# Key and query products put in runs of one array shape in two attention stages, and two constants stored as full tiles

## The chip, the cores and the metric

The kernel runs on one core of a Trainium2 chip. The metric is the device time of one execution in microseconds, lower is better. The engines are named as in the profile: PE is TensorE's matmul, PEld its weight load (the stationary operand), DVE VectorE, ACT ScalarE, POOL GpSimd, and SP the engine that issues most DMAs. The arrays are float32. Where the code splits a value into a high and a low part of type float32r, it multiplies these parts separately and adds the products.

## The reference

Two transformer layers for 512 tokens of width 1024. The first is a hybrid of a neighbourhood attention (8 heads of 64), a bidirectional gated delta rule (4 heads of 128), an output projection and a mixture of 64 experts. The second joins an mLSTM (4 heads of 256), a short convolution, a stick-breaking attention (16 heads of 64), gates, and an MLP of width 4096. The two parts that the change is about, cut to what matters:

```python
def row_block(args):                       # neighbourhood attention, one row of the grid
    r, q_row = args
    r0 = jnp.clip(r - kh // 2, 0, rows - kh)
    k_win = lax.dynamic_slice_in_dim(kg, r0, kh, axis=0)[:, :, :, col_idx]
    v_win = lax.dynamic_slice_in_dim(vg, r0, kh, axis=0)[:, :, :, col_idx]
    logits = jnp.einsum('bhqd,rbhqcd->bhqrc', q_row, k_win) * scale + bias
    p = jax.nn.softmax(logits.reshape(b_, h_, GRID_W, kh * WIN_W), axis=-1)
    return jnp.einsum('bhqrc,rbhqce->bqhe', p.reshape(b_, h_, GRID_W, kh, WIN_W), v_win)

def block(args):                           # stick-breaking attention, one block of queries
    qblk, start = args
    mask = key_pos[None, :] < q_pos[:, None]
    z = jnp.einsum('bhqd,bshd->bhqs', qblk, kf)
    log_beta = jax.nn.log_sigmoid(z)
    log_1m = jnp.where(mask, log_beta - z, 0.0)
    cum = jnp.cumsum(log_1m, axis=-1)
    a = jnp.where(mask, jnp.exp(log_beta + cum[..., -1:] - cum), 0.0)
    return jnp.einsum('bhqs,bshd->bqhd', a, vf)
```

## The kernel before

The program runs through the layers in order: input projections, the delta rule's preparation, the neighbourhood attention together with the delta rule's scan, the output projection and the routing, the experts, and then the second layer. Most of the work is dense projections, which the text calls jobs: weights come by DMA into a ring of buffers, ACT and DVE split them into a high and a low part (lines 160 and 161), and PE makes 24 matmuls of 128x512 for each block of 128 output columns (`fm_mm`, line 255).

**Who sets the order.** A scheduler orders the instructions on each engine's queue, from the order in the program and its own estimate of when operands are ready. Where the code says `manual_schedule` for PE, PE's queue keeps the program's order. The stick-breaking stage is such a place; the neighbourhood attention is not. In both, a generator of small steps is mixed with another one by hand: `pad` takes a step's figure as the amount of dense work to place behind it. In the stick-breaking stage, dense jobs (line 255) are put between the steps of `sb_group`, six jobs for each group of two pairs, eight for the last. In the neighbourhood attention the steps of `na_attn` are put between those of the scan, `dn_scan` (its matmuls are on lines 1023 to 1125).

**Neighbourhood attention** (`na_attn`, `na_pair`, `na_out`, lines 711 to 797). There are four blocks of 128 queries and eight heads, taken in pairs: 16 calls of `na_pair`, two of them in flight at a time. A block sees two or three blocks of keys (`nb`), so a head's logits have 256 or 384 columns; two of the four blocks have each. The queries and keys of the pair's two heads lie in the partitions 0 to 63 and 64 to 127 of the same tiles. For each head the kernel makes the product of queries and keys (line 743: 64 rows contracted, float32, which PE carries out as two instructions), adds the mask as a product with the identity (line 747: 128 rows, bfloat16), and reads the sum with the bias on DVE (line 750). Then come the exponentials on ACT (759), transposes (767), and the products with the values (775). The logits' accumulators are taken from `pacc`, which has four; the scan takes its own from the same four.

**Stick-breaking** (`sb_stack`, `sb_pair`, lines 1838 to 1927). The 16 heads are taken in eight pairs. For a pair the low and high parts of the queries and keys are stacked: `Q` holds, for each head e, the high part of the queries in its own 64 partitions and the low part in the other 64; `K` the high part of the keys in both; `Kl` the low part of the keys, head 0 in partitions 0 to 63 and head 1 in 64 to 127. So one product of 128 rows (line 1868) gives high times high plus high times low, and one of 64 rows (line 1870) the third term. The logits z of a head are triangular and lie in four regions of 512, 384, 256 and 128 columns, in three accumulators for each head:

```python
for i in range(4):
    b, c, n = self.REG[i]
    for e in range(2):
        o = slice(64 * e, 64 * e + 64)
        ks = slice(i * 128, i * 128 + 128)
        TE.matmul(z[e][b][:, c:c + n], K[:, e, ks], Q[:, e, i * 128:512],
                  start=(i != 3), stop=False, skip_group_check=True)
        TE.matmul(z[e][b][:, c:c + n], Kl[o, ks], Q[o, e, i * 128:512],
                  start=False, stop=False, skip_group_check=True)
```

These 16 matmuls are followed by eight of the causal mask (line 1875, bfloat16, 128 columns each). Then ACT and DVE work out the softplus and split it (lines 1880 to 1893; the low half of `sb_hl` is made on line 1887), with dense jobs on PE meanwhile, and line 1904 (eight matmuls with the triangle `ntri`), 1908 to 1913 (with the constant `none`) and 1923 (with the values) follow for each head.

**Constants** (`b2_consts`). `oner` holds ones and `none` minus ones. Both are one column of 128 partitions, and are read as a stationary operand of 128x128 by a broadcast along the free axis. `none` is used on lines 1908 to 1913 (128 products) and `oner` on line 2065 for the accumulator `ml_pd` (32 products); the same line makes `ml_pn` with a full tile as the stationary operand.

Of the kernel before, what the change touches and what calls it, by code (L numbers as in the profile page):

```python
# [10 lines left out]
F32 = mybir.dt.float32  # L11
F32R = mybir.dt.float32r
# [4 lines left out]
OP = mybir.AluOpType  # L17
# [6 lines left out]
NEG = -1.0e30  # L24
# [57 lines left out]
class Kern:  # L82
# [648 lines left out]
    def na_pair(self, cb, g, block, po, sm):  # L731
        TE, VE, SE, na = self.TE, self.VE, self.SE, self.na
        kb0, nb, (s0, st) = block
        mx = na.tile([128, 2], F32, name="na_mx", tag="na_mx", bufs=2)
        lps, es, pTs = [], [], []
        v = lambda a: a.rearrange("p (r k) -> p r k", r=8)
        for i in range(2):
            h = 2 * g + i
            hp, o = h // 2, 64 * (h % 2)
            lp = na.tile([128, 384], F32, name="na_lp", tag="na_lp", bufs=3)[:, :nb * 128]  # L740
            pl = self.pacc.tile([128, 384], F32, name="na_l", tag=self.atag)[:, :nb * 128]

            TE.matmul(pl, self.qT[o:o + 64, hp, cb, :],
                      self.kT[o:o + 64, hp, kb0 * 128:(kb0 + nb) * 128]
                      .rearrange("p (n r k) -> p r n k", n=nb, r=8), start=True, stop=False)
            mk = self.mk[:, None, s0:s0 + st * (nb - 1) + 1:st, :].to_broadcast([128, 8, nb, 16])
            TE.matmul(pl, self.idb, mk, start=False, stop=True)
            base = self.braw[:, h, 16 * (kb0 - cb + 1):16 * (kb0 - cb + 1) + 1]
            bias = bass.AP(tensor=base.tensor, offset=base.offset, ap=[list(base.ap[0]), [31, 8], [1, 16 * nb]])
            VE.tensor_tensor_reduce(out=v(lp), in0=v(pl), in1=bias, scale=1.0, scalar=NEG,  # L750
                                    op0=OP.add, op1=OP.max, accum_out=mx[:, i:i + 1])
            lps.append(lp)
            if i == 0:
                yield 0.3 * nb
        VE.tensor_scalar(mx, mx, -1.0, None, op0=OP.mult)
        for i in range(2):

            e = na.tile([128, 384], F32, name="na_e", tag="na_e", bufs=4)
            SE.activation(e[:, :nb * 128].rearrange("p (n r k) -> p r n k", n=nb, r=8),
                          lps[i].rearrange("p (r n k) -> p r n k", n=nb, r=8), AF.Exp, bias=mx[:, i:i + 1],  # L760
                          accum_out=sm[:, 2 * g + i:2 * g + i + 1])
            es.append(e)
        yield 0.3 * nb
        for i in range(2):
            pt = self.psm.tile([128, 3, 128], F32, name="na_pt", tag="ps")
            for b in range(nb):
                TE.transpose(pt[:, b, :], es[i][:, b * 128:(b + 1) * 128], self.ident)
            pT = na.tile([128, 3, 128], F32, name="na_pT", tag="na_pT", bufs=2)
            self.copy(pT[:, :nb, :], pt[:, :nb, :], "vs"[i])
            pTs.append(pT)  # L770
            yield 0.1 * nb
        for i in range(2):
            h = 2 * g + i
            for b in range(nb):
                TE.matmul(po[:, h, :], pTs[i][:, b, :], self.V[:, kb0 + b, h * 64:(h + 1) * 64],
                          start=(b == 0), stop=(b == nb - 1))
            yield 0.2 * nb
# [907 lines left out]
    def b2_consts(self, p, sb):  # L1685
        VE = self.VE

        def r(name, fn, dt=BF16, p=p):
            t = p.tile([128, 128], dt, name=name)
            fn(t)  # L1690
            return t
        self.ntri = r("ntri", lambda t: VE.tensor_scalar(t, self.le, -1.0, None, op0=OP.mult), F32R, sb)
        oner = p.tile([128, 1], F32R, name="oner")
        VE.tensor_copy(oner, self.ones[:, 0:1])
        self.oner = oner.to_broadcast([128, 128])
        none = sb.tile([128, 1], F32R, name="none")
        VE.tensor_scalar(none, self.ones[:, 0:1], -1.0, None, op0=OP.mult)
        self.none = none.to_broadcast([128, 128])
        self.idr = r("idr", lambda t: VE.tensor_copy(t, self.ident))

        self.m_le = r("m_le", lambda t: VE.tensor_scalar(t, self.le, -2.0 ** 100, None, op0=OP.mult), BF16, sb)
        self.m_lt = r("m_lt", lambda t: VE.tensor_scalar(t, self.ge, 2.0 ** 100, -2.0 ** 100, op0=OP.mult, op1=OP.add))
        self.epsc = p.tile([128, 1], F32, name="epsc")
        VE.memset(self.epsc, EPS)
        self.bif = p.tile([4, 2], F32, name="bif")
        for i in range(2):
            self.GE.dma_start(self.bif[:, i:i + 1], self.A["b_if_2"][4 * i:4 * i + 4].rearrange("(a b) -> a b", b=1))
# [148 lines left out]
    def sb_pair(self, hp):  # L1856
        TE, VE, SE, GE, sb = self.TE, self.VE, self.SE, self.GE, self.sb
        self.sb_stack(hp)
        Q, K, Kl = self.sbt.pop(("s", hp))
        v = self.sbt.pop(("v", hp))  # L1860
        self.catch_up()
        z = [self.zregions("sb_z") for _ in range(2)]
        for i in range(4):
            b, c, n = self.REG[i]
            for e in range(2):
                o = slice(64 * e, 64 * e + 64)
                ks = slice(i * 128, i * 128 + 128)
                TE.matmul(z[e][b][:, c:c + n], K[:, e, ks], Q[:, e, i * 128:512],  # L1868
                          start=(i != 3), stop=False, skip_group_check=True)
                TE.matmul(z[e][b][:, c:c + n], Kl[o, ks], Q[o, e, i * 128:512],  # L1870
                          start=False, stop=False, skip_group_check=True)
        for e in range(2):
            for i in range(4):
                b, c, n = self.REG[i]
                TE.matmul(z[e][b][:, c:c + 128], self.idr, self.m_le, start=False, stop=False, skip_group_check=True)  # L1875
        sp = []
        for e in range(2):
            t = sb.tile([128, 1280], F32, name="sb_t", tag="sb_t", bufs=2)
# [10 lines left out]
            f, g = self.FLAT[2], self.FLAT[3]  # L1889
# [8 lines left out]
        for e in range(2):  # L1898
            t, hl, sm = sp[e]
            for i in range(4):  # L1900
                b, c, n = self.REG[i]
                f = self.FLAT[i]
                for a in range(2):
                    TE.matmul(z[e][b][:, c:c + n], self.ntri, hl[:, a, f:f + n],  # L1904
                              start=False, stop=(i == 3 and a == 1), skip_group_check=True)
            f, g = self.FLAT[1], self.FLAT[3]
# [12 lines left out]
# [3 lines that stand above are left out]
                n = 512 - 128 * i  # L1922
                TE.matmul(po[o, 512 - n:512], v[:, i, o], aa[e][:, self.FLAT[i]:self.FLAT[i] + n],  # L1923
                          start=(i == 0), stop=(i == 3))
# [267 lines left out]
```

## Time and profile before

| | |
|---|---|
| median of three runs | 2284.15 us (2281.66 to 2285.14) |
| the profiled execution's own time | 2290.18 us |
| its span, first to last instruction | 2288.4 us |
| mean granted TensorE clock over the span | 0.976 |
| instructions in the span | 27538 |
| HBM read and written | 336.61 MB and 22.02 MB |

The span is cut into 40 slices in the page's second part, so a slice is 57.2 us. Rows of a timeline give the start and the length in us; several equal instructions in a row are merged and counted (x8). A matmul's length reaches past the start of the next one, because matmuls are pipelined: what it costs PE is read from start to start. The form `64*128 64x512` is a stationary operand of 64 rows by 128 columns and a moving one of 64 rows by 512. A window's row has its length, then for each of PE, PEld, DVE, ACT and POOL the busy us and the number of instructions, then the granted clock (1.00 is 2.4 GHz, 0.50 is 1.2 GHz), the DMA share and GB/s.

### The profile page before, as it was taken

To read this page: it belongs to the slowest core of one execution; us is meant where nothing else is said; L and a number is where in the kernel's file an instruction comes from. 1 tells how busy PE (TensorE), PEld (TensorE's weight loads), DVE (VectorE), ACT (ScalarE), POOL (GpSimd) and SP (SyncE) were. 2 spreads that over 40 slices of the span, in tenths; PEclk is the share of its full clock that TensorE was granted. 3 is DMA by queue.
4 is the path that set the end of the run, shared out by engine and by line. 5 is a ranking of instruction groups with operands and counts; after the bars stand their busy time and mean duration, and the time that the engine had idled before them with its cause. 6 is when DMAs were issued, how large, how long until landed. Compare 5 with 4: busy or idle time off the path is not lost.

```text
span 2288.4 us, 27538 instructions
## 1 busy us (share of the span) xinstructions
PE 2196.5 (96%) x11333; PEld 1659.2 (73%) x11333; DVE 999.3 (44%) x1622; ACT 783.0 (34%) x1245; POOL 146.0 (6%) x171
## 2 busy tenths in 40 slices
PE   6989999899999999779999999999999999999998
PEld 4867787755555555357777788888888888888887
DVE  5479667521111111253555444555344444534333
ACT  3545543211111111134565524444322342423222
POOL 1020001000000000011122000000000000000000
PEclk9999999999999999888999999999999999999999
DMA  6212100789999999912111222222233322323322
GB/s 186 73 57 74 57 2 19 268 283 413 412 410 412 399 394 409 351 56 63 56 43 51 74 75 79 81 79 74 92 102 99 104 92 83 111 92 98 105 92 74
DMA packets 175397, 348.71 MB, mean 152 GB/s; under 512 B 15604, under 2 KB 115037, under 8 KB 167075
## 3 DMA queue, kind: packets, MB, share of 16 engines
q1 hardware_dynamic: 169827, 339.25, 41.6%
q0 software_dynamic: 4592, 4.50, 0.6%
q10 hardware_dynamic: 848, 3.15, 0.4%
q8 instruction: 91, 1.49, 0.3%
q14 instruction: 39, 0.32, 0.0%
HBM read 336.61 MB, written 22.02 MB: 157 GB/s over the span
## 4 chain that ended last, share of the span: by engine, by line
PE 56%; DVE 1%; ACT 0%; issue 0%; DMA 0%; POOLq 0%; POOL 0%; ACTq 0%
PE acc L255 37%; PE acc L305 8%; PE acc L332 2%; PE acc L214 2%; PE sb_z L1870 1%; PE sb_z L1868 1%; PE sb_o L1923 1%; PE sb_z L1904 1%; PE ml_s L2045 1%; PE ml_pn L2065 1%; PE pv L1825 0%; PE sb_z L1908 0%; PE n_ps L443 0%; PE sb_z L1875 0%; PE ml_pd L2065 0%; PE sb_z L1912 0%
## 5 line engine op out<-in xcount | busy, mean ns | idle before, releaser
L255 PE MATMUL acc<-hT,hl_fm 128*128 128x512 f32 x3504 | 829.9, 396 | 2.1 <-DVE hl_fm L161 2.0
L255 PEld LDWEIGHTS acc<-hT,hl_fm 128*128 128x128 f32 x3504 | 660.7, 190 | 142.8 <-issue 3.8
L161 DVE TENSOR_TENSOR hl_fm<-rawA,hl_fm 128x1024 fp32r<-128x1024 f32 x176 | 217.4, 1235 | 145.8 <-ACT hl_fm L160 145.6
L160 ACT CAST hl_fm<-rawA 128x1024 fp32r<-128x1024 f32 x176 | 184.6, 1050 | 269.4 <-PE acc L255 201.1
L1449 PE MATMUL gu<-rawB,XT 128*64 128x512 f32 x528 | 186.2, 609 | 12.8 <-DMA rawB<-in_expert_w_up_dram 12.5
L305 PE MATMUL acc<-hl_tm,uT 128*128 128x512 f32 x672 | 152.8, 389 | 0.0
L305 PEld LDWEIGHTS acc<-hl_tm,uT 128*128 128x128 f32 x672 | 126.1, 188 | 26.2
L1457 DVE TENSOR_TENSOR hd<-sg,gu 128x256 f32<-128x256 f32 x32 | 13.5, 421 | 274.8 <-ACT sg L1455 274.8
L1426 PEld LDWEIGHTS g_ps<-oneh,h 128*128 128x128 f32 x960 | 115.5, 188 | 23.6 <-issue 16.2
L1426 PE MATMUL g_ps<-oneh,h 128*128 128x256 f32 x960 | 121.7, 284 | 0.0
L1449 PEld LDWEIGHTS gu<-rawB,XT 128*64 128x64 f32 x528 | 57.9, 139 | 82.6 <-issue 72.2
L1485 ACT ACTIVATE obs<-dn_o,slots 128x512 f32<-128x512 f32 x60 | 41.2, 687 | 194.5 <-PE dn_o L1482 188.1
L1482 PE MATMUL dn_o<-rawB,ht 128*64 128x512 f32 x280 | 102.3, 605 | 1.6 <-DVE x L1501 1.6
L1449 PE MATMUL gu<-rawH,XT 128*64 128x512 f32 x208 | 94.3, 596 | 1.3 <-DMA rawH<-in_expert_w_up_dram 0.8
L161 DVE TENSOR_TENSOR hl_tm<-rawA,hl_tm 128x1024 fp32r<-128x1024 f32 x48 | 58.8, 1224 | 67.2 <-ACT hl_tm L160 67.1
L255 PE MATMUL acc<-yA,hl_fm 128*128 128x512 f32 x384 | 87.4, 389 | 0.0
L255 PEld LDWEIGHTS acc<-yA,hl_fm 128*128 128x128 f32 x384 | 72.1, 188 | 15.0
L160 ACT CAST hl_tm<-rawA 128x1024 fp32r<-128x1024 f32 x48 | 50.3, 1048 | 95.2 <-PE acc L305 86.4
L305 PE MATMUL acc<-hl_tm,hT 128*128 128x512 f32 x288 | 74.6, 413 | 0.0
L1449 PE MATMUL gu<-rawC,XT 128*64 128x512 f32 x152 | 70.5, 605 | 1.2 <-DMA rawC<-in_expert_w_up_dram 1.1
L305 PEld LDWEIGHTS acc<-hl_tm,hT 128*128 128x128 f32 x288 | 55.5, 198 | 11.1
L1440 ACT ACTIVATE XT<-g_ps,g 128x256 f32<-128x256 f32 x64 | 26.8, 470 | 106.0 <-PE g_ps L1426 100.6
(511 smaller groups left out, 2931.6 us busy)
## 6 DMA issues: line engine op xcount, KB each, us to landing
rawA<-in_w_in_dram SPq DMA_DIRECT2D x66, 1024.0 KB
rawB<-in_expert_w_down_dram SPq DMA_DIRECT2D x35, 1024.0 KB
rawB<-in_expert_w_gate_dram SPq DMA_DIRECT2D x66, 512.0 KB
rawB<-in_expert_w_up_dram SPq DMA_DIRECT2D x66, 512.0 KB
rawA<-in_w_up_dram SPq DMA_DIRECT2D x16, 1024.0 KB
rawA<-in_w_down_dram SPq DMA_DIRECT2D x16, 1024.0 KB
rawH<-in_expert_w_down_dram SPq DMA_DIRECT2D x13, 1024.0 KB
rawH<-in_expert_w_gate_dram SPq DMA_DIRECT2D x26, 512.0 KB
```

Of the source, the lines that this page charges most:

```text
L160: self.SE.copy(hi, src)
L161: self.VE.tensor_sub(lo, src, hi.bitcast(F32))
L214: self.TE.matmul(p[:, t:t + 256], j[4][:, a, k, :], h[:, b, k, t:t + 256], start=(t == 0 and i == 0), stop=(t > 0 and i == 23), skip_group ...
L255: self.TE.matmul(ps, hl[:, a, k, :], h[:, b, k, :], start=(n == 0), stop=(n == 23))
L305: self.TE.matmul(ps, h[:, a, k, c * 128:(c + 1) * 128], hl[:, b, kk, :], start=(first and n == 0), stop=(last and n == 5))
L332: self.TE.matmul(ps, h[:, a, k, c * 128:(c + 1) * 128], st["w"][:, b, k, :], start=(n == 0), stop=(n == 23))
L1426: TE.matmul(ps[:, k % 2, :], self.h2[:, a, c, k * 128:(k + 1) * 128], oh[:, c].rearrange("p e s -> p (e s)"), start=(n == 0), stop=(n == 7))
L1440: self.SE.activation(xt[:, 2 + j, :], ps[:, j, :], AF.Copy, scale=self.g2[:, 2 * i + j:2 * i + j + 1])
L1449: TE.matmul(pg[64 * e:64 * e + 64, :], xt[k // 4][:, k % 4, o:o + 64], w[k // 4 * 2 + e].rearrange("p (i j c) -> p i j c", i=2, j=4)[:, :, ...
L1482: TE.matmul(po[64 * e:64 * e + 64, :], ht[:, j, 64 * e:64 * e + 64], w[e].rearrange("p (j c) -> p j c", j=2)[:, j, s], start=(j == 0), sto ...
L1485: SE.activation(ob[:, s], po, AF.Copy, scale=sl[:, 1:2])
L1868: TE.matmul(z[e][b][:, c:c + n], K[:, e, ks], Q[:, e, i * 128:512], start=(i != 3), stop=False, skip_group_check=True)
```

## The change

Three edits. In `na_pair`, both accumulators are taken first, the two heads' query-key products are issued one behind the other, then the two mask products, and the reads on DVE follow; the step that stood between the heads now stands behind both, with the same figure. In `b2_consts`, `oner` and `none` become tiles of 128x128. In `sb_pair`, the loop over the regions is split in two: first the eight 128-row products, then the eight 64-row ones, in which the two heads alternate.

```diff
@@ -734,24 +734,25 @@
         mx = na.tile([128, 2], F32, name="na_mx", tag="na_mx", bufs=2)
         lps, es, pTs = [], [], []
         v = lambda a: a.rearrange("p (r k) -> p r k", r=8)
+        mk = self.mk[:, None, s0:s0 + st * (nb - 1) + 1:st, :].to_broadcast([128, 8, nb, 16])
+        pls = [self.pacc.tile([128, 384], F32, name="na_l", tag=self.atag)[:, :nb * 128] for _ in range(2)]
+        for i in range(2):
+
+            o = 64 * i
+            TE.matmul(pls[i], self.qT[o:o + 64, g, cb, :],
+                      self.kT[o:o + 64, g, kb0 * 128:(kb0 + nb) * 128]
+                      .rearrange("p (n r k) -> p r n k", n=nb, r=8), start=True, stop=False)
+        for i in range(2):
+            TE.matmul(pls[i], self.idb, mk, start=False, stop=True)
         for i in range(2):
             h = 2 * g + i
-            hp, o = h // 2, 64 * (h % 2)
             lp = na.tile([128, 384], F32, name="na_lp", tag="na_lp", bufs=3)[:, :nb * 128]
-            pl = self.pacc.tile([128, 384], F32, name="na_l", tag=self.atag)[:, :nb * 128]
-
-            TE.matmul(pl, self.qT[o:o + 64, hp, cb, :],
-                      self.kT[o:o + 64, hp, kb0 * 128:(kb0 + nb) * 128]
-                      .rearrange("p (n r k) -> p r n k", n=nb, r=8), start=True, stop=False)
-            mk = self.mk[:, None, s0:s0 + st * (nb - 1) + 1:st, :].to_broadcast([128, 8, nb, 16])
-            TE.matmul(pl, self.idb, mk, start=False, stop=True)
             base = self.braw[:, h, 16 * (kb0 - cb + 1):16 * (kb0 - cb + 1) + 1]
             bias = bass.AP(tensor=base.tensor, offset=base.offset, ap=[list(base.ap[0]), [31, 8], [1, 16 * nb]])
-            VE.tensor_tensor_reduce(out=v(lp), in0=v(pl), in1=bias, scale=1.0, scalar=NEG,
+            VE.tensor_tensor_reduce(out=v(lp), in0=v(pls[i]), in1=bias, scale=1.0, scalar=NEG,
                                     op0=OP.add, op1=OP.max, accum_out=mx[:, i:i + 1])
             lps.append(lp)
-            if i == 0:
-                yield 0.3 * nb
+        yield 0.3 * nb
         VE.tensor_scalar(mx, mx, -1.0, None, op0=OP.mult)
         for i in range(2):
 
@@ -1690,12 +1691,8 @@
             fn(t)
             return t
         self.ntri = r("ntri", lambda t: VE.tensor_scalar(t, self.le, -1.0, None, op0=OP.mult), F32R, sb)
-        oner = p.tile([128, 1], F32R, name="oner")
-        VE.tensor_copy(oner, self.ones[:, 0:1])
-        self.oner = oner.to_broadcast([128, 128])
-        none = sb.tile([128, 1], F32R, name="none")
-        VE.tensor_scalar(none, self.ones[:, 0:1], -1.0, None, op0=OP.mult)
-        self.none = none.to_broadcast([128, 128])
+        self.oner = r("oner", lambda t: VE.tensor_copy(t, self.ones), F32R)
+        self.none = r("none", lambda t: VE.tensor_scalar(t, self.ones, -1.0, None, op0=OP.mult), F32R, sb)
         self.idr = r("idr", lambda t: VE.tensor_copy(t, self.ident))
 
         self.m_le = r("m_le", lambda t: VE.tensor_scalar(t, self.le, -2.0 ** 100, None, op0=OP.mult), BF16, sb)
@@ -1863,11 +1860,14 @@
         for i in range(4):
             b, c, n = self.REG[i]
             for e in range(2):
+                TE.matmul(z[e][b][:, c:c + n], K[:, e, i * 128:i * 128 + 128], Q[:, e, i * 128:512],
+                          start=(i != 3), stop=False, skip_group_check=True)
+
+        for i in range(4):
+            b, c, n = self.REG[i]
+            for e in range(2):
                 o = slice(64 * e, 64 * e + 64)
-                ks = slice(i * 128, i * 128 + 128)
-                TE.matmul(z[e][b][:, c:c + n], K[:, e, ks], Q[:, e, i * 128:512],
-                          start=(i != 3), stop=False, skip_group_check=True)
-                TE.matmul(z[e][b][:, c:c + n], Kl[o, ks], Q[o, e, i * 128:512],
+                TE.matmul(z[e][b][:, c:c + n], Kl[o, i * 128:i * 128 + 128], Q[o, e, i * 128:512],
                           start=False, stop=False, skip_group_check=True)
         for e in range(2):
             for i in range(4):
```

## Rows read from the trace of the kernel before

**Rows 1.** The page's busy shares, and its slices: the granted clock

```profile
PE 2196.5 (96%) x11333; PEld 1659.2 (73%) x11333; DVE 999.3 (44%) x1622; ACT 783.0 (34%) x1245; POOL 146.0 (6%) x171
...
PEclk9999999999999999888999999999999999999999
```

**Rows 2.** Waits of PE, 1039 to 1295 us: total us, times, longest

```profile
PE pv L1825 <- ACT sb_vT L1814: 0.7, 1, 0.7
```

**Rows 3.** Windows of the eight groups: us, engines' busy us, clock, DMA

```profile
1041.16:1047.12 5.96, 5.96 (x19) 3.27 (x18) 1.82 (x2) 0.48 (x1) 0.11 (x1) 0.88 0.05 15
...
1107.30:1112.74 5.44, 5.44 (x19) 2.93 (x18) 1.29 (x2) 0.28 (x1) 0.12 (x1) 1.00 0.00 0
...
1230.73:1236.18 5.45, 5.45 (x19) 2.93 (x17) 1.29 (x2) 0.28 (x1) 0.11 (x1) 1.00 0.00 0
...
sum 45.24, PE 45.24 PEld 24.05 DVE 5.69 ACT 1.31 POOL 0.99; mean PE 5.65 PEld 3.01 DVE 0.71 ACT 0.16 POOL 0.12
```

**Rows 4.** Timeline of PE, the third group: start us, us, line, matmul, count

```profile
1107.30 0.47 PE L1868 MATMUL sb_z<-sb_Q,sb_K 128*128 128x512 f32 x1
1107.70 0.50 PE L1870 MATMUL sb_z<-sb_Q,sb_Kl 64*128 64x512 f32 x1
```

**Rows 5.** Timeline of PE behind the third group, L1904 and what follows

```profile
1125.53 1.38 PE L1904 MATMUL sb_z<-sb_hl,ntri 128*128 128x512 f32 x8
1126.75 0.56 PE L1908 MATMUL sb_z<-sb_hl,none 128*128 128x384 f32 x2
```

**Rows 6.** Windows of the five stretches at a lower clock

```profile
1045.68:1052.50 6.82, 6.82 (x23) 5.39 (x24) 2.48 (x4) 5.27 (x9) 3.85 (x4) 0.50 0.00 0
...
1236.83:1240.23 3.40, 3.40 (x9) 2.62 (x9) 2.25 (x3) 3.40 (x8) 3.14 (x3) 0.50 0.00 0
sum 23.83, PE 23.83 PEld 18.67 DVE 10.95 ACT 17.92 POOL 16.60; mean PE 4.77 PEld 3.73 DVE 2.19 ACT 3.58 POOL 3.32
```

**Rows 7.** Windows from a group's end to L1904, first and third pair

```profile
1047.12:1062.43 15.31, 15.31 (x63) 12.59 (x63) 10.84 (x14) 11.45 (x17) 4.94 (x6) 0.82 0.03 4
1112.74:1125.53 12.79, 12.79 (x63) 10.65 (x63) 9.79 (x13) 11.45 (x17) 4.93 (x6) 1.00 0.01 1
```

**Rows 8.** Timeline of PE in the mixture of experts, column halves

```profile
600.40 0.59 PE L1449 MATMUL gu<-rawA,XT 128*64 128x512 f32 x1
600.41 0.59 PE L1449 MATMUL gu<-rawC,XT 128*64 128x512 f32 x1
600.83 0.59 PE L1449 MATMUL gu<-rawA,XT 128*64 128x512 f32 x1
```

**Rows 9.** Timeline of DVE behind the third group, L1887

```profile
1121.25 1.49 DVE L1887 TENSOR_TENSOR sb_hl<-sb_t,sb_hl 128x1280 fp32r<-128x1280 f32 x1
```

**Rows 10.** Line groups of PE by shape, L2065: busy us, mean ns

```profile
L2065 PE MATMUL ml_pn<-ml_Ps,ml_v 128*128 128x512 f32 x24 | 6.8, 393 | 0.0
...
L2065 PE MATMUL ml_pd<-ml_Ps,oner 128*128 128x512 f32 x8 | 2.5, 394 | 0.0
```

**Rows 11.** Timeline of PE in the neighbourhood attention

```profile
284.09 0.91 PE L743 MATMUL na_l<-kv,qT 64*128 64x384 f32 x2
...
285.42 0.33 PE L747 MATMUL na_l<-bm_m,idb 128*128 128x384 bf16 x1
...
290.72 0.91 PE L743 MATMUL na_l<-kv,qT 64*128 64x384 f32 x2
291.56 0.34 PE L747 MATMUL na_l<-bm_m,idb 128*128 128x384 bf16 x1
291.83 0.91 PE L743 MATMUL na_l<-kv,qT 64*128 64x384 f32 x2
```

**Rows 12.** The attention stretch: its window, and waits of PE and DVE

```profile
262.00:365.00 103.00, 102.83 (x795) 83.13 (x794) 63.54 (x183) 44.62 (x130) 6.76 (x11) 1.00 0.04 12
...
PE sc_vn L1077 <- DVE sc_r L1070: 1.5, 1, 1.5
...
DVE na_lp L750 <- PE na_l L747: 13.3, 14, 2.2
```

## The prediction

> **What bounds the kernel now.** I read the busy shares and the slices first. TensorE (PE) is busy 96% of the span, and its granted clock is 9 tenths or more nearly everywhere, with a dip to 8 in three slices about the middle [rows 1]. The change touches two stretches: the neighbourhood attention (262 to 365 us) and the stick-breaking heads, "sb" (1039 to 1295 us), where the dip is. In the sb stretch the waits list has a single wait of PE, 0.7 us long [rows 2]: there, time that PE saves is time saved. So what is read next is PE's own spacing, from one matmul's start to the next, because the durations overlap.
>
> Each of the eight sb pairs starts with 16 key-query products, 45.24 us in all, 5.44 us for a pair whose clock is full [rows 3]. Inside, a 128-row product (L1868) and a 64-row one (L1870) alternate; at 512 columns the second starts 0.40 us behind the first [rows 4]. A run of the same widths in one shape, L1904, needs 1.22 us for eight [rows 5]: 0.15 us each on average, against 5.44/16 = 0.34 here. The 0.19 us between them is paid at every change of shape, and it is more than half of the group.
>
> The clock comes next. In five stretches of sb, 23.83 us together, it is granted at 0.50, so 1.2 of 2.4 GHz [rows 6]. The first begins inside a group, the last 0.65 us behind one (1236.83 against 1236.18), and the other three inside the second, fourth and sixth group [rows 3, 6]; what PE did before each fall was these products. From the end of a group to L1904 the same 63 instructions take 15.31 us behind the first and 12.79 us behind the third, which ran at 1.00 [rows 7].
>
> **Step 1, sb products grouped.** Per pair: eight 128-row products in one run, 1.22 us [rows 5]. Then eight 64-row ones, of which neighbours now lie in opposite partition halves and write different tiles of z. Whether two row halves run side by side, no row shows. The nearest row divides the array by columns: L1449's two halves start 0.01 us apart, and the next follow 0.42 us behind, so two cost one [rows 8]. That gives 0.61 us; the other end, one after the other, is 1.22. I take 0.61, since the nearest row too is a split of the array in two. Two changes of shape stay, 0.38 us. Sum: 1.22 + 0.61 + 0.38 = 2.21 us, times 8 = 17.7, so 45.24 - 17.7 = **27.5 us** less. At the serial end it is 2.82 x 8 = 22.6, so 22.6 less.
>
> The row divides columns, and of row tiles the Trainium skill is less generous: "TensorE: Matmul & The Clock Gate", Measured speedup vs the span model, has four of them run 3.07 times as fast, not 4. An estimate from that page is 1.5 times for two, 0.8 us in place of 0.61, and a step of 26.0 us. No run here shows it.
>
> **Step 2, the clock.** It follows from step 1 if the alternation is what lowers it. Of the 23.83 us, 5.5 lie inside the groups (1.44 of them in the first, 1045.68 to 1047.12), and their loss is in step 1 already. The other 18.3 lie over dense work, where a microsecond of them costs (15.31 - 12.79) / (1052.50 - 1047.12) = 0.47 us [rows 6, 7]: **8.6 us**. The ends are 0 and 8.6. I take 8.6: with a group of 2.2 us, half of it in the spacing of dense work, little is left of what stood ahead of every fall, and three of the eight groups have none behind them even now, the third among them [rows 7].
>
> What could be late next is VectorE: the low halves of sb_hl, which L1904 reads, are ready at 1122.74 (L1887), and L1904 starts at 1125.53 [rows 5, 9]. That path runs from the end of the group, as before, and this is a pair that has full clock already, so 2.8 us of slack stay. A small edge goes with it: the next pair's Q and K tiles come free as much earlier as the group ends.
>
> **Step 3, full-tile constants.** The product with broadcast ones (L2065, ml_pd) and the same line with a full stationary tile (ml_pn) take 394 and 393 ns at 512 columns [rows 10]. The broadcast costs nothing that can be seen, so the gain is 0; some 160 such products at 1 ns either way are 0.2 us. Filling two full tiles on VectorE in place of two columns lies under PE's dense work: 0. Without that cover it is under 0.3 us: L1887 does ten times a tile's elements in 1.49 [rows 9].
>
> **Step 4, neighbourhood attention.** A head's product is two 64-row instructions, at 384 columns 0.84 us to the next start (290.72 to 291.56). Of this 2 x 0.32 is streaming (0.42 x 384/512 from [rows 8]), and 0.20 the change of shape behind it; ahead of it lie about 0.09 more (it starts 0.27 us behind the mask product of the same width, whose own streaming, at half of 0.32, with a like overhead is 0.18) [rows 11]. So a head costs 0.93 us, and 0.72 at 256 columns, of which 0.29 is going in and out of the shape. There are 16 pairs, half of each width. If both heads run side by side, one of each pair disappears: 8 x 0.93 + 8 x 0.72 = 13.2 us. If they only stand next to each other, 16 x 0.29 = 4.7. If PE's order keeps them apart, 0. That order isn't written by hand, and it already puts a head's product and its mask apart (L743 at 284.09, L747 at 285.42) [rows 11]. I take three quarters of 13.2, less 2 us at the stage's end, where PE waits 1.5 us for the scan (L1077) [rows 12]: **8 us**.
>
> The moved step claims two of the four accumulators ahead of its first product. Behind a late one on PE stand the scan's products (L1068, L1077, L1089, same pool), and VectorE's L750 for the first head comes a head's product later. VectorE is busy 63.5 of 103 us and itself waits 13.3 us for these products, while PE is busy 102.8 [rows 12]: nothing beyond the 2 us. No transfer moves; both stretches' loads are issued by other queues.
>
> **Sum.** 27.5 + 8.6 + 0 + 8 = **44 us**. The profiled execution's 2290.2 us becomes 2246; the median shown, 2284.15, stands 6.0 lower, and 44 off it is **2240 us**.
>
> **Rivals.** The **64-row halves don't overlap**: for it, that no row shows two row halves together; against it, the column halves. 22.6 + 8.6 + 3.5 (three quarters of 4.7) = 34.7, so 2249.5. Chance 0.20.
>
> The **clock falls all the same**, for there is still switching in each group: 27.5 + 8 = 35.5, so 2248.7. Chance 0.12; together with the first rival 22.6 + 3.5 = 26, so 2258, 0.04.
>
> **Attention gives nothing**, because PE's order keeps the heads apart, or PE waits for VectorE in place of the switch: 36, so 2248. Chance 0.13.
>
> **Slower**: the pair's hold on two of four accumulators makes the scan's products wait, and the scan is a chain of four steps on which the stage's end hangs. To come out slower by over 0.2% it must eat the 36 us of steps 1 and 2 and 4.6 more, 41 us over 16 pairs, from 2.5 us a pair on: 2289 or more. Against it: the longest wait of PE in that stage is 1.5 us [rows 12]. Chance 0.03.
>
> The **grouping does nothing**: the 0.19 us belongs to these products themselves (the same Q and K tiles read again and again), not to the change of shape, in attention too: 0 us, 2284. For it, that no row shows two 64-row products in a run; against it, that L1904, in one shape, isn't held up [rows 5]. Chance 0.03.
>
> **How the numbers follow.** The forecast itself has 0.45. A difference of 0.2%, 4.6 us, is about what a measurement of this kernel can tell from no change. All cases but the last two lie 26 us or more below: faster 0.94, same 0.03, slower 0.03. The range goes from all of step 4 (49 in place of 44, and 3.5 for the spread of the runs: 2231) up to 2256, the dearest single rival and the 6 us by which the profiled execution stands off the median. Outside stay the double rival, the last two, and tails.
>
> **What would show it.** In sb, L1868's eight in some 1.2 us, then L1870's in pairs 0.01 us apart, groups of 2.2 us (2.8 if serial); the granted clock at 1.00 through the stage, and 12.8 us from a group to L1904. In attention, L743 of both heads starting together. L2065 unchanged. The forecast is wrong if the groups stay over 3 us, if L1904 begins to wait for VectorE, or if the attention stage gets no shorter though its products do.

## The result, and the profile after

The changed kernel takes 2247.23 us, the median of four runs (2244.26 to 2249.74), against 2282.9 for the kernel before (2278.37 to 2285.14). The ratio is 0.9846, interval 0.9826 to 0.9866, so 35.7 us less (30.6 to 39.7 by the interval). The forecast was 2240, its range 2231 to 2256. Profiled against profiled it is 2290.18 to 2247.45, 42.7 us.

**The sb groups.** Windows of the same eight groups, columns as in [rows 3]:

```profile
1033.73:1035.92 2.19, 2.19 (x20) 1.91 (x18) 1.82 (x2) 0.49 (x1) 0.50 (x1) 1.00 0.12 40
1062.70:1064.80 2.10, 2.10 (x18) 1.82 (x16) 0.00 (x0) 0.00 (x0) 0.58 (x1) 1.00 1.05 368
1087.49:1090.44 2.95, 2.42 (x19) 1.91 (x17) 1.29 (x2) 0.28 (x1) 0.60 (x1) 1.00 0.00 0
...
sum 19.44, PE 17.85 PEld 14.90 DVE 5.69 ACT 1.33 POOL 4.04; mean PE 2.23 PEld 1.86 DVE 0.71 ACT 0.17 POOL 0.50
```

The second kind returns in the fourth, sixth and eighth group, the third kind in the fifth and seventh. So 45.24 us [rows 3] became 19.44. PE's timeline of the fourth group, as in [rows 4] (eight products of one kind are merged into one row):

```profile
1117.22 1.38 PE L1863 MATMUL sb_z<-sb_Q,sb_K 128*128 128x512 f32 x8
1118.54 0.85 PE L1870 MATMUL sb_z<-sb_Q,sb_Kl 64*128 64x512 f32 x8
1119.32 0.40 PE L1875 MATMUL sb_z<-m_le,idr 128*128 128x128 bf16 x4
```

From start to start, eight 128-row products and the change of shape behind them take 1.32 us, and eight 64-row ones 0.78 with the change back; taken one by one, the 64-row ones start in pairs 3 to 4 ns apart. The halves overlap.

The third, fifth and seventh group hold something new. PE's waits from 1030 to 1255 us, and the timeline of the third group (in brackets the idle time before a row, and what ended it):

```profile
PE sb_z L1863 <- DVE yA L1684: 1.6, 3, 0.5
PE pv L1822 <- ACT sb_vT L1811: 0.7, 1, 0.7
```

```profile
1087.49 1.19 PE L1863 MATMUL sb_z<-sb_Q,sb_K 128*128 128x512 f32 x5
1089.21 0.53 PE L1863 MATMUL sb_z<-sb_Q,sb_K 128*128 128x256 f32 x3 [0.53 <-DVE yA L1684]
1089.66 0.85 PE L1870 MATMUL sb_z<-sb_Q,sb_Kl 64*128 64x512 f32 x8
```

DVE, in the same stretch:

```profile
1087.77 0.69 DVE L1824 COPY sb_v<-pv 128x512 f32<-128x512 f32 x1 [3.05 <-PE pv L1822]
1088.38 0.68 DVE L1684 TENSOR_TENSOR yA<-sb_o,yA 128x512 fp32r<-128x512 f32 x1
```

The sixth 128-row product needs an accumulator that DVE's L1684 (the low half of yA) still reads. L1684 is queued behind a copy of v that itself waits for PE. Alternating, PE came to this accumulator 3.8 us into the group (1111.09 in the third group of before); grouped, the sixth product starts 0.9 us into a group that doesn't wait. PE idles 0.53 us, and the product ahead of the wait runs out with nothing over it, so the group takes 2.95 us in place of 2.10: 3 x 0.85 = 2.6 us are given back.

**The clock.** Windows of the whole sb stage, from its first group to its last output product, before and after:

```profile
1041.16:1293.52 252.36, 252.36 (x1190) 192.78 (x1189) 128.53 (x155) 142.76 (x226) 49.56 (x60) 0.95 0.16 51
```

```profile
1033.73:1252.09 218.36, 216.77 (x1190) 177.21 (x1189) 129.82 (x155) 142.37 (x226) 44.70 (x60) 1.00 0.19 59
```

The granted clock is 1.00 throughout, and the stage is 34.0 us shorter. From a group's end to L1904 it is 12.78 us behind the first pair as behind the third, where [rows 7] had 15.31 and 12.79:

```profile
1035.92:1048.70 12.78, 12.78 (x67) 10.65 (x63) 9.78 (x13) 11.45 (x17) 4.48 (x6) 1.00 0.00 0
1090.44:1103.22 12.78, 12.78 (x67) 10.66 (x63) 10.07 (x13) 11.45 (x17) 3.92 (x5) 1.00 0.00 1
```

Outside the groups the stage took 252.36 - 45.24 = 207.1 us before and 218.36 - 19.44 = 198.9 after: the clock gave 8.2 us there.

**The attention.** PE's timeline where two heads stand together:

```profile
291.24 0.92 PE L742 MATMUL na_l<-kv,qT 64*128 64x384 f32 x4
292.09 0.50 PE L746 MATMUL na_l<-bm_m,idb 128*128 128x384 bf16 x2
```

Four products, both heads, take 0.85 us to the next start, as long as one head's two took before [rows 11]. In nine of the 16 pairs the heads stand together on PE, in seven the scheduler has put something between them.

What PE saved is read from the whole stretch between the first neighbourhood product and the first expert product (gu): first the kernel before in its second profile (below), then the changed kernel. Both have 6.8 us at half clock in it:

```profile
264.69:458.05 193.36, 182.03 (x1225) 150.49 (x1223) 125.61 (x349) 73.06 (x167) 15.11 (x24) 0.98 0.27 98
```

```profile
266.06:455.95 189.89, 175.97 (x1224) 148.46 (x1222) 124.60 (x349) 72.65 (x167) 15.09 (x24) 0.98 0.28 103
```

PE is busy 6.1 us less and idle 2.6 us more, so the stretch is 3.5 us shorter. The same stretch takes 193.32 us in `const_only` and 193.36 in `sb_regions`, which lack the attention part, and 189.98 in `fix_yA`, which has it (all below, each with 6.8 us at half clock). The waits of PE in it that involve attention and scan, changed kernel first:

```profile
PE do_t L1144 <- DVE do_sq L1141: 2.2, 2, 1.3
PE na_py L794 <- DVE na_at L791: 1.7, 4, 0.6
PE sc_vn L1078 <- DVE sc_r L1071: 1.5, 1, 1.5
PE acc L305 <- DVE yna L554: 0.8, 1, 0.8
PE na_pt L768 <- ACT na_e L760: 0.3, 1, 0.3
```

```profile
PE sc_vn L1077 <- DVE sc_r L1070: 1.5, 1, 1.5
PE do_t L1143 <- DVE do_sq L1140: 1.4, 2, 0.9
PE acc L305 <- DVE yna L554: 0.6, 1, 0.6
PE na_py L793 <- DVE na_at L790: 0.5, 2, 0.3
```

These are 6.5 us of waits for 4.0.

**The constants.** The lines of [rows 10], after: 394 and 396 ns for 393 and 394.

```profile
L2065 PE MATMUL ml_pn<-ml_Ps,ml_v 128*128 128x512 f32 x24 | 6.9, 394 | 0.0
...
L2065 PE MATMUL ml_pd<-ml_Ps,oner 128*128 128x512 f32 x8 | 2.5, 396 | 0.0
```

### The profile page after: what moved, and what is told of

Read it like the earlier page. It is cut to its first block, busy times and chain, and to the rows that moved or that the text cites. A ratio compares the mean times of both kernels' runs of the same rounds, so it can differ in the third digit from the quotient of the medians.

```text
span 2245.7 us, 27540 instructions
## 1 busy us (share of the span) xinstructions
PE 2151.2 (96%) x11333; PEld 1639.4 (73%) x11333; DVE 999.0 (44%) x1622; ACT 782.2 (35%) x1245; POOL 141.1 (6%) x171
## 4 chain that ended last, share of the span: by engine, by line
PE 55%; DVE 1%; ACT 0%; issue 0%; DMA 0%; POOLq 0%; POOL 0%; ACTq 0%
PE acc L255 38%; PE acc L305 8%; PE acc L332 2%; PE acc L214 2%; PE sb_o L1923 1%; PE sb_z L1904 1%; PE ml_s L2045 1%; PE ml_pn L2065 1%; PE pv L1822 0%; PE sb_z L1863 0%; PE sb_z L1908 0%; PE sb_z L1870 0%; PE n_ps L443 0%; PE ml_pd L2065 0%; PE sb_z L1912 0%
```

## The experiments

**One part at a time.** Three kernels have one part of the change each, and the kernel before was profiled once more.

`sb_only`: the kernel before, with this part of the diff alone (cut, with comments added):

```
+        for i in range(4):   # all K products
...
+        for i in range(4):   # then all Kl products, heads side by side
```

> The kernel before with the stick-breaking products alone put in runs of one shape. If the gain comes from the changes of shape and the clock, as forecast, the sb stretch (first sb_z product to last sb_o) is 34 us shorter than in the profiled execution of before, as in the changed kernel, the granted clock is 1.00 in it, three groups hold a wait for yA near 0.86 us, and the time is 27 to 34 us below before. If the parts only work together, or attention carries most of it, it is under 22 us below.

2247.83 us (2245.11 to 2250.68), 0.9832 of before (0.9799 to 0.9865). Its second and third group and its stage:

```profile
1064.85:1066.95 2.10, 2.10 (x17) 1.81 (x15) 0.00 (x0) 0.00 (x0) 0.59 (x1) 1.00 1.06 372
1089.60:1092.56 2.96, 2.42 (x19) 1.91 (x17) 1.29 (x2) 0.28 (x1) 0.60 (x1) 1.00 0.00 0
...
1035.91:1253.99 218.08, 216.47 (x1190) 176.98 (x1189) 129.76 (x155) 142.26 (x226) 44.72 (x60) 1.00 0.19 59
```

The grouping alone gives the groups, the full clock and the new wait of the whole change, and nearly the whole gain: 34.3 us of 35.7.

`na_only`: the attention part alone (two accumulators per pair, both heads' products, then both masks).

> The kernel before with the neighbourhood attention alone changed. Forecast's mechanism: 9 of the 16 pairs stand next to each other on PE's queue and overlap, the attention stretch ends 5 to 7 us sooner, and the time is 5 to 9 us below before. Rival: the stretch's gain is lost in the experts, which wait for weights: less than 2 us.

2278.86 us (2274.82 to 2283.29), 0.9983 (0.9966 to 1.0): at the edge of what can be told. Its median is 3.3 us below that of before (2282.17), short of the 5 to 9 that were expected. Its stretch from the first neighbourhood product to the first expert product is 3.4 us shorter than in the second profile of before, as in the changed kernel:

```profile
265.50:455.43 189.93, 175.85 (x1225) 148.75 (x1224) 124.70 (x349) 72.84 (x167) 15.09 (x24) 0.98 0.28 100
```

`const_only`: the full-tile constants alone.

> The kernel before with oner and none as full tiles alone. Forecast: no difference that can be measured (within 2 us), the spacing of L1908 to L1913 and of L2065 unchanged within 5 ns. Rival: a broadcast stationary operand loads more slowly than the durations show; then 160 products gain 20 ns or more each, 3 us or more.

2285.57 us (2276.98 to 2288.05), 1.0005 (0.999 to 1.0021). No difference can be measured.

`before_again`: the kernel before, nothing edited.

> The kernel before, unchanged, profiled once more. The profiled execution of before took 2290.2 us while its other runs have a median of 2282.9. If the half-clock stretches of the sb stage differ from execution to execution, this profile has fewer than 23.8 us of them there and a time nearer 2283, and time and mean clock of the runs go together. If they are fixed, it has again about 23.8 us there and the 7 us lie elsewhere.

2281.26 us, 0.9986 (0.9968 to 1.0004) of the kernel before itself; this profiled execution took 2284.61, 5.6 less than the first one. Neither branch of the expectation fits whole: in sb the half clock did change, but this profile has more of it, 27.3 us for 23.83 [rows 6], and the difference in time lies earlier. Windows from 255 to 500 us, first profile of before, then the second, then the changed kernel:

```profile
255.00:500.00 245.00, 233.44 (x1670) 181.24 (x1670) 141.55 (x393) 84.12 (x187) 16.22 (x25) 0.96 0.34 122
```

```profile
255.00:500.00 245.00, 233.67 (x1711) 181.19 (x1710) 142.17 (x395) 85.37 (x189) 17.23 (x26) 0.99 0.37 132
```

```profile
255.00:500.00 245.00, 231.08 (x1728) 181.06 (x1728) 141.69 (x396) 86.69 (x192) 17.20 (x26) 0.99 0.37 135
```

The first profile granted 0.96 there (20.5 us at half clock), the second 0.99 (6.8 us), and the first expert product starts at 463.0 and 458.0. At the 0.47 us that a microsecond of half clock cost in sb, 13.7 of them would be 6.4 us; the first expert products are 4.9 apart, and the first profile stood 6.0 off the median. All four profiles of kernels that alternate have 17 to 27 us of half clock in sb; the changed kernel and `sb_only` have none.

**What the grouping is made of.** `sb_onehalf` is `sb_only` with the 64-row products head by head, so that neighbours on the queue lie in the same half:

```
-        for i in range(4):
-            for e in range(2):
+        for e in range(2):
+            for i in range(4):
                 ...
                 TE.matmul(z[e][b][:, c:c + n], Kl[o, i * 128:i * 128 + 128], Q[o, e, i * 128:512],
```

> The kernel before, the stick-breaking products grouped as in the change, but the eight 64-row products head by head, so that neighbours lie in the same partition half. If the overlap of opposite halves is what makes them cheap, a group without a wait takes 2.7 to 2.9 us in place of 2.10, and its 64-row products start 0.06 to 0.23 us apart. If one shape alone is enough, it stays at 2.1 to 2.2 us.

2253.84 us in a single run (before: 2282.78). The groups did not get longer. The second one's window; then PE's timeline there, followed by two short cuts of it, 1069.45 to 1069.60 and 1069.80 to 1069.90 us:

```profile
1068.17:1070.27 2.10, 2.10 (x18) 1.84 (x16) 0.00 (x0) 0.00 (x0) 0.59 (x1) 1.00 1.07 376
```

```profile
1069.47 0.86 PE L1873 MATMUL sb_z<-sb_Q,sb_Kl 64*128 64x512 f32 x8
1070.27 0.34 PE L1878 MATMUL sb_z<-m_le,idr 128*128 128x128 bf16 x3
...
1069.47 0.51 PE L1873 MATMUL sb_z<-sb_Q,sb_Kl 64*128 64x512 f32 x2
...
1069.47 0.69 PE L1873 MATMUL sb_z<-sb_Q,sb_Kl 64*128 64x512 f32 x4
```

Two products have started by 1069.60 and four by 1069.90. Taken one by one, the first two have 512 columns and start 14 ns apart, although on the queue the widths of one head (512, 384, 256, 128) stand ahead of the second 512. The eight still take 0.80 us. So the halves overlap in this order too, and this kernel could not serve as the serial case: the rival that the halves don't overlap falls by the groups themselves, not by an experiment that makes them serial. The 6 us by which this run is above `sb_only` are not the order's price: its sb stage is 217.91 us for 218.08, and from 255 to 500 us it has 20.5 us at half clock, as the first profile of before had.

`sb_regions` is `sb_only` with the two loops made one again, but in the order K, K, Kl, Kl for each region: eight runs of one shape in a group where the grouped order has two, six more changes.

> The kernel before, with two 128-row products and then the two 64-row ones for each of the four regions: eight changes of shape in a group in place of sixteen, and the halves overlap. If each change of shape costs near 0.2 us, a group takes 3.0 to 3.4 us; if the cost is that of the 64-row products and not of the change, about 2.2 us, as in the changed kernel. If the clock falls whenever a group switches at all, the sb stretch keeps some half-clock time; if it takes the long alternation, it has none.

2252.37 us in a single run. Its second group, the sum over all eight, and its sb stage:

```profile
1060.77:1064.06 3.29, 3.29 (x18) 1.84 (x16) 0.00 (x0) 0.00 (x0) 0.06 (x1) 1.00 0.72 250
...
sum 26.57, PE 26.57 PEld 15.00 DVE 5.68 ACT 1.31 POOL 0.53; mean PE 3.32 PEld 1.87 DVE 0.71 ACT 0.16 POOL 0.07
...
1030.68:1255.73 225.05, 225.05 (x1191) 177.10 (x1189) 127.73 (x155) 142.21 (x226) 47.94 (x60) 1.00 0.19 57
```

(3.29 - 2.10) / 6 = 0.20 us for each change of shape, the price that [rows 4, 5] gave. With it the saving of a whole group adds up: 14 changes at 0.20 and 0.61 for the halves side by side are 3.4 us, and 5.44 - 2.10 is 3.34. Outside the groups the stage is 225.05 - 26.57 = 198.5 us, as short as with the full grouping, at a clock of 1.00. So the clock stayed up with half of the alternation left: in the kernel before it fell in or behind five of eight groups of 16 runs of one shape in 5.4 us, here behind none of eight groups of eight runs in 3.3. Whether the number of changes counts or the time that goes into them, the two kernels don't tell apart. And PE does not wait for yA here.

**Can the new wait be taken away?** `fix_yA` is the changed kernel with the product that waits, and its mask, behind the other seven (cut):

```
+        order = [(i, e) for i in (0, 1, 3) for e in range(2)] + [(2, 0)]
+        for i, e in order: hi(i, e)
+        for i, e in order: mask(i, e)
+        hi(2, 1)
+        mask(2, 1)
```

> The changed kernel, with the product that needs the accumulator last freed (the second head's third region) put behind seven of the eight mask products. If the wait for yA before the fourth pair's products is what makes three groups 0.86 us longer, they fall to within 0.3 us of the others, the sb stretch loses 2 to 2.5 us, and the time is 1 to 3 us below the changed kernel's 2247, 36 to 38 below before. Rival: the wait moves to the next instruction and nothing is gained.

2249.9 us (2245.36 to 2250.74), 0.9841 (0.9798 to 0.9885): no better than the change, whose 2247.23 lies in that spread. With the masks in, the third group takes 2.86 us (3.38 in the changed kernel), but new waits have come, 1030 to 1262 us:

```profile
PE acc L255 <- DVE merged L1939: 2.3, 1, 2.3
PE acc L255 <- ACT sb_k L1816: 1.2, 3, 0.4
```

The 2.3 us are a product of the dense layer that comes to its accumulator before DVE has emptied it. DVE around it:

```profile
1210.04 1.24 DVE L1892 CAST sb_hl<-sb_t 128x1280 fp32r<-128x1280 f32 x1
1211.21 0.68 DVE L1939 TENSOR_SCALAR merged<-acc 128x512 f32<-128x512 f32 x1
```

L1939 had to stand behind the splitting of sb_hl. Behind that wait the granted clock is 0.54 in a window of 3.7 us:

```profile
1212.50:1216.20 3.70, 3.70 (x13) 3.15 (x12) 3.65 (x4) 1.94 (x4) 1.37 (x1) 0.54 0.16 20
```

The whole stage, as it was shown for the changed kernel (218.36 us, PE busy 216.77):

```profile
1030.90:1255.03 224.13, 220.58 (x1191) 179.09 (x1189) 128.17 (x155) 143.00 (x226) 53.12 (x60) 0.99 0.19 57
```

It is 5.8 us longer, where 2 to 2.5 less were expected. The yA wait was real and could be moved, and what it held back met the next one: the rival of the expectation.

**Does the scheduler's order in the attention cost the missing gain?** `na_manual` is the changed kernel with PE's instructions of attention and scan in the order of the program:

```
-        pad(self.na_attn(), self.dn_scan())
+        with tc.manual_schedule(engines={mybir.EngineType.PE}):
+            pad(self.na_attn(), self.dn_scan())
```

> The changed kernel, with PE's queue in program order through the attention and the scan, so that all 16 pairs stand next to each other. If the shortfall of the attention comes from the seven pairs that the scheduler keeps apart, the stretch to the last sc_o gets 3 to 6 us shorter than in the changed kernel. If it comes from the scan's last step, which waits for its own chain behind the attention, it gets no shorter, and an order that isn't planned may make PE wait more, 5 us or longer.

2283.21 us (2279.98 to 2287.29), 0.9999 of before (0.9981 to 1.0017): the whole 36 us are lost again. All 16 pairs now stand together, and yet the waits of PE from 272 to 424 us are

```profile
PE do_t L1145 <- DVE do_sq L1142: 14.7, 3, 5.5
PE na_py L795 <- DVE na_at L792: 12.0, 4, 3.1
PE na_o L777 <- DVE na_pT L106: 7.2, 8, 1.7
```

and the clock falls. The stretch from its first neighbourhood product to the scan's last one, then the same in the changed kernel:

```profile
272.25:423.28 151.03, 112.88 (x784) 97.27 (x784) 78.21 (x223) 49.55 (x138) 10.55 (x15) 0.86 0.02 5
```

```profile
266.06:377.65 111.59, 106.58 (x850) 90.69 (x849) 75.95 (x222) 49.36 (x140) 9.31 (x14) 1.00 0.04 11
```

The kernel is a blunt tool, since it also takes away the scheduler's mixing of attention with the scan. So it doesn't tell what the seven pairs that stand apart cost. It shows that heads standing together aren't enough: in the order of the program PE waits 33.9 us for DVE on the three lines above, where the changed kernel, with the scheduler's mixing, waits 3.9 on do_t and na_py.

## Why the prediction was right, and where it was off

**Step 1: right mechanism, 25.8 us for 27.5.** A group was put at 2.21 us and takes 2.10 to 2.19 where nothing waits. The halves overlap fully (0.78 us for eight with a change of shape, against 0.61 + 0.19 forecast), and a change of shape costs 0.20 (`sb_regions`). From the Trainium skill, "TensorE: Matmul & The Clock Gate", Measured speedup vs the span model, the prediction worked out an estimate of 0.8 us for the halves; the row goes with the 0.61. The missing 1.7 us is the 2.6 that the three waiting groups give back, less what the groups came out shorter. The prediction looked for "what could be late next" in sb_hl, which never was late; it didn't ask who still holds the accumulators that the 128-row products now open earlier.

**Step 2: right, about 8.2 us for 8.6.** The half clock is gone with the grouping alone (`sb_only`) and the dense stretch takes the 12.8 us that was forecast. `sb_regions` narrows the cause to the long alternation: half as many changes, in groups of 3.3 us, leave the clock at 1.00. Which of the two does it stays open. Steps 1 and 2 together are the 34.0 us by which the stage is shorter, for 36.1.

**Step 3: right, nothing** (`const_only`).

**Step 4: this term was mis-sized, 3.5 us for 8.** Side by side the products cost what was forecast. The 8 us were three quarters of 13.2, that is 9.9, less 2 for waits. But nine of the 16 pairs stand together, four at 384 columns and five at 256, not three quarters: at the forecast's own prices (0.93 and 0.72) that is 7.3, and PE's busy time in the stretch fell by 6.1. Of these, 2.6 became idle time in place of the 2 taken off. It isn't the scan's wait (sc_vn), which stays 1.5 us, that grew: PE now comes too early to na_py and do_t, which wait for DVE. So the largest miss is the "three quarters", a share that no row had shown. By its time (2248) the rival "attention gives nothing" is nearest, and both of its reasons, the order and the waits for VectorE, took a part; but the part gave 3.5 us and not nothing.

**The sum and where it was taken off.** The measured parts, 25.8 + 8.2 + 0 + 3.5, are 37.5 us, and the medians differ by 35.7, with an interval that holds both. Against the profiled execution the forecast's 44 looks almost met (42.7), but only because that execution had lost some 5 us between 255 and 500 us, where its clock was lower, which the change has no part in: `before_again` is 4.9 us earlier at the first expert product with the same code. Taking the whole 44 off the median moved the error there. The range held because its upper end went by the dearest rival and 6 us more, which was room for a mis-sized step 4.

**The other rivals.** The halves do overlap, the clock doesn't fall, the grouping does do something. The pair's hold on two of the four accumulators made no wait of the scan that the list shows, so "slower" didn't begin to come true.

## What to carry to other kernels

Where TensorE is busy and never waits, read the spacing from start to start by shape: matmuls of another shape in between cost 0.20 us a change here, and runs of one shape, with 64-row products in opposite halves, take that away. The same edit brings each accumulator into use earlier, so list who reads it last and what stands ahead of that reader on its engine. Price a saving in a stage that hangs on a chain by the stage's end, not by the engine's busy time (6.1 us saved, 3.5 kept), and compare two profiles of the same kernel before you take one execution's clock for the kernel's.

## What the hardware showed that was not expected

Products in opposite 64-row halves ran side by side even when one half's four stood ahead of the other's on the queue (`sb_onehalf`: starts 14 ns apart at 512 columns, 0.80 us for all eight, 0.80 in `sb_only`). The Trainium skill, "TensorE: Matmul & The Clock Gate", Part 3, says that matmuls start and end in the order of the program; the trace's starts don't fit that here, and the unchanged length of the group speaks for the trace.

PE's half clock came in sb with hardly any idle time of PE before it: in [rows 2] the stage has one wait of 0.7 us, ahead of the first group, and five stretches at 0.50 [rows 6]. Each began inside a group of alternating shapes or 0.65 us behind one, though three of the eight groups had no fall. With eight changes of shape in a group in place of 16, in 3.3 us in place of 5.4, the clock stayed at 1.00.
